# Second-sort sums, payloads and bucket comparisons in other places of a 32-slot neighbour-sum kernel, and two results turned by TensorE

## The chip, the cores and the metric

The kernel runs on one core of a Trainium2 chip. The metric is the device time of one execution in microseconds (us). Engines are called TensorE (PE in the profile; its weight loads are PEld), VectorE (DVE), ScalarE (ACT), GpSimd (POOL) and SyncE (SP).

## The reference, cut to what matters

```python
num_nodes, num_edges, dim = 4096, 65536, 128
output = np.zeros((num_nodes, dim), dtype=np.float32)
for i in range(len(edge_index_src)):
    output[edge_index_dst[i]] += node_features[edge_index_src[i]]
```

Every edge adds the feature row of its source node to the row of its destination node.

## The kernel before, in words

The nodes are 32 blocks of 128. The edges are sorted twice on the chip by prefix counts and permutation matmuls: a first sort by destination block, and then a second sort by source block inside each destination block. The second sort is done for 8 groups g = 0 to 7 of four destination blocks. The main loop has 32 slots; slots 4g to 4g+3 belong to group g, and each takes eight of the 32 source blocks.

**A slot.** VectorE writes one-hot matrices `oh` of low source and low destination numbers one slot ahead (`onehots(slot+1)`, L241), in two buffers. TensorE multiplies them into eight blocks `psa`, each of which counts the edges from one source block to the group's 512 destination nodes (L806, two halves of 16 matmuls), ScalarE casts each block to SBUF as `a` (L808), and TensorE multiplies features by `a` into the result bank `pso` (L813, eight products with k 0 to 3 in the slot itself, eight with k 4 to 7 in the next slot). TensorE's order in a slot is: first half of the blocks; place 2; the late products of the slot before; second half of the blocks; places 3 and 4; the early products; `finish`; place 5. VectorE's order is: place 0; the one-hots of the next slot; place 1; the later places. In slots before 5 the one-hots come in two halves, later in one.

**Hooks.** `at(slot, place, functions)` hangs the second sort's steps of a group into those places, by hand. Each engine runs what it is handed in this order, so a step that waits holds all that was handed to its engine after it. For a group g of 3 and up, with f = 4g:

- `buckets` (VectorE, L633): one-hot of the source block. `chunk_sums` (GpSimd, L653): adds it up in twos and fours, into `two` and `four`. The payloads that are owed by group g-1 (GpSimd, L642) follow.
- `before_all` (TensorE, L662, three matmuls into `psb`; ScalarE copies it out as `base`, L664): the sums ahead of each bucket. It reads `four`.
- `masked` and `folded` (GpSimd, L689, L696, L698): reads `base`.
- `payloads` (GpSimd, L642), by `LATE_PAYLOADS` here or owed to the next group.
- `repeats` (VectorE, L669, L675) and `repeats_folded` (GpSimd, L684).
- `ranks` (TensorE L706, ScalarE L710), which reads what `folded` and `repeats_folded` left; `permutations` (VectorE, L241, tiles `p2a` for even and `p2c` for odd groups); `permuted` (TensorE, L722); `quad_keys` (VectorE, L529).

Groups 1 and 2 have places of their own: group 2's `buckets` and `chunk_sums` stand inside `onehots(0)`, and its `before_all`, `masked` and `folded` in slot 0, behind `x_part(3, 1)` (GpSimd, L230).

**Results.** A result of four destination blocks is complete in slot 4k+4. ScalarE copies it from `pso` to the PSUM bank `misc` (`psx`, L376), VectorE transposes it in squares of 32 (`finish`, L390), and SyncE's queue stores it with four DMAs that put the squares in place. The last result goes out by `leave` (L397). The bank `misc` also takes `psb`; the bank `ps2` takes the ranks and the permuted pairs.

Of the kernel before, what the change touches and what calls it, by code (L numbers as in the profile page):

```python
# [8 lines left out]
P = 128  # L9
F32 = mybir.dt.float32  # L10
# [15 lines left out]
BIG = 4096.0  # L26
GROUPS = (4,) * 8
WARM = 38
LATE_PAYLOADS = (2, 3, 4, 5)

WIN = ((0, 4, 0, 44), (4, 9, 0, 72), (9, 13, 8, 92), (13, 17, 16, 112), (17, NJ, 28, P))

# [44 lines left out]
def _fast(ctx, tc, X, src32, dst32, out, ident, fmax, flag_i, T):  # L77
    nc = tc.nc
    V, S, G, PE = nc.vector, nc.scalar, nc.gpsimd, nc.tensor
# [3 lines left out]
    sb1 = ctx.enter_context(tc.tile_pool(name="sb1", bufs=1))  # L83
    sb2 = ctx.enter_context(tc.tile_pool(name="sb2", bufs=2))
    ps = ctx.enter_context(tc.tile_pool(name="ps", bufs=2, space=bass.MemoryType.PSUM))
# [12 lines left out]
    for a, b in runs:  # L98
        at, n = 8 * sum(QN[:a]), 4 * QN[a]
        for queue, of, to in ((nc.sync, dst32, rawd), (nc.scalar, src32, raws)):  # L100
            queue.dma_start(
                out=to.rearrange("p (q n) w -> p q n w", q=NQ)[:, a:b, :n],
                in_=bass.AP(of, at, [[2 * T, P], [2 * n, b - a], [2, n], [1, 2]]))
# [119 lines left out]
    def x_part(i, v, hs=(0, 1)):  # L223
        blks = slice(i % 2 * BX, (i % 2 + 1) * BX)
        if v == 0:
            S.copy(out=xr[i // 2][:, blks, 0, :], in_=xf[i])
        else:
            for h in hs:
                bs = slice(i % 2 * BX + h * BX // 2, i % 2 * BX + (h + 1) * BX // 2)
                G.tensor_tensor(out=xr[i // 2][:, bs, 1, :], op=OP.subtract,  # L230
                                in0=xf[i][:, h * BX // 2:(h + 1) * BX // 2],
                                in1=xr[i // 2][:, bs, 0, :])
# [139 lines left out]
    done = []  # L372

    def evacuate(k, pso):
        res = ps.tile([P, 512], F32, name="psx", tag="misc", bufs=1)
        S.copy(out=res[:], in_=pso[:])  # L376
        done.append((k, res))

    def store_blocks(queues, rows, k):

        for a in range(4):
            queues[a % len(queues)].dma_start(
                out=out[4 * k * P:4 * (k + 1) * P, 32 * a:32 * (a + 1)].rearrange(
                    "(b j) f -> j b f", j=32),
                in_=rows[32 * a:32 * (a + 1)].rearrange("p (b f) -> p b f", f=32))

    def finish():
        for k, res in done:
            rows = sb2.tile([P, 512], F32, name="rows", bufs=1)
            V.transpose(out=rows[:], in_=res[:])  # L390
            store_blocks((nc.sync,), rows, k)
        done.clear()

    def leave(k, pso):
# [206 lines left out]
    owed = {}  # L601
    hooks = {}

    def at(slot, where, *fs):
        hooks.setdefault((slot, where), []).extend(fs)

    def do(slot, where):
        for f in hooks.pop((slot, where), ()):
            f()

    def pass2(g):
# [43 lines left out]

        def before_all():
            T2["b"] = sb2.tile([P, 2, P], BF16, name="base2")
            psb = ps.tile([P, 512], F32, name="psb", tag="misc", bufs=1)
            of = T2["four"][:].rearrange("p (h i) w -> p h i w", h=2)
            n = NH // 4  # L660
            for i in range(n):
                PE.matmul(out=psb[:, :2 * P], lhsT=before[:], rhs=of[:, :, i],  # L662
                          start=i == 0, stop=i == n - 1)
            S.copy(out=T2["b"][:].rearrange("p h w -> p (h w)"), in_=psb[:, :2 * P])  # L664
# [48 lines left out]
        def permutations(j):  # L713
            pair_onehot(p2b[d0 // 2 % 4 + j], T2["r"][:, j], slice(0, NCH))

        def permuted(j):
            if j == 0:
                T2["ps2"] = ps.tile([P, 512], F32, name="ps2", tag="ps2", bufs=1)
            ps2 = T2["ps2"]
            for c in range(NCH):  # L720
                at = (c // NH * 2 + j) * 64
                PE.matmul(out=ps2[:, at:at + 64], lhsT=p2b[d0 // 2 % 4 + j][:, c, :],  # L722
                          rhs=T2["v"][:, c, :, 2 * j:2 * j + 2],
                          start=c % NH == 0, stop=c % NH == NH - 1)
            if j == 1:
                take_pairs(ps2[:, 8 * NB:8 * NB + P], ps2[:, :8 * NB])
# [32 lines left out]
        def each(*fs):  # L759
            return lambda: [f() for f in fs]  # L760
# [5 lines left out]
            return buckets, payloads, column_sums, sums_to_each, counts  # L766
        if g == 2:
            owed[2] = payloads
            at(1, 1, repeats, repeats_folded)
            at(4, 3, ranks, lambda: permutations(0), lambda: permutations(1))  # L770
            at(5, 3, lambda: permuted(0))
            at(5, 5, lambda: permuted(1))
            at(7, 0, quad_keys)
            return buckets, chunk_sums, before_all, each(masked, folded)
        f = 4 * g
        where = 4 if g == 3 else 1
        at(f - 10, where, buckets, chunk_sums, owed.pop(g - 1, lambda: None))
        at(f - 9, 5, before_all)
        at(f - 8, where, masked, folded)
        if g in LATE_PAYLOADS:  # L780
            owed[g] = payloads
        else:
            at(f - 8, where, payloads)
        at(f - 6, 1, repeats, repeats_folded)
        at(f - 4, 5, ranks)
        at(f - 3, 1, lambda: permutations(0), lambda: permutations(1))
        at(f - 3, 5, lambda: permuted(0), lambda: permuted(1))
# [2 lines left out]
    def onehots(slot):  # L790

        oh = sb1.tile([P, 2, 4 * 8, P], BF16, name="oh", tag=f"t2{slot % 2}")
        at = slot % 4 * 32
        parts = ((0, 16), (16, 16)) if slot < 5 else ((0, 32),)
        for i, n in ((0, 8), (8, 8), (16, 16)) if slot == 0 else parts:
            if i == 16 and slot == 0:
                buckets_2()
                chunk_sums_2()
            for k, io in ((0, piotas), (1, piota)):
                onehot(oh[:, k, i:i + n], keys2[slot // 4][k][:, at + i:at + i + n], n, io=io)  # L800
        return oh

    def blocks(k, oh, a):
        psa = ps.tile([P, 512], F32, name="psa", tag="psA", bufs=4)
        for i in range(4):
            PE.matmul(out=psa[:, i * P:(i + 1) * P], lhsT=oh[:, 0, 4 * k + i, :],  # L806
                      rhs=oh[:, 1, 4 * k + i, :], start=True, stop=True)
        S.copy(out=a[:, k, :], in_=psa[:])  # L808

    def product(k, slot, a, pso):  # L810
        s = slot % 4 * 8 + k
        for v in range(2):
            PE.matmul(out=pso[:], lhsT=xr[s // 16][:, s % 16, v, :], rhs=a[:, k, :],  # L813
                      start=s == 0 and v == 0, stop=s == NB - 1 and v == 1)
# [16 lines left out]
    def flag_of_all(fall):  # L831
        psf = ps.tile([P, 512], F32, name="psf", tag="misc", bufs=1)
        PE.matmul(out=psf[:1, :1], lhsT=fall[:], rhs=one[:], start=True, stop=True)
        V.tensor_single_scalar(out=flag_i[:], in_=psf[:1, :1], scalar=float(P * T),
                               op=OP.not_equal)

    buckets_1, payloads_1, column_sums_1, sums_1, counts_1 = pass2(1)
    buckets_2, chunk_sums_2, before_all_2, masked_counts_2 = pass2(2)
    for g in range(3, len(GROUPS)):
        pass2(g)  # L840

    V.tensor_copy(out=earlier[:, :, :4 * (NH - 1)].bitcast(F32),
                  in_=ones[:, :4 * (NH - 1)].bitcast(F32)[:, None].to_broadcast([P, 2, 2 * (NH - 1)]))
# [39 lines left out]
    for slot in range(slots):  # L883
        do(slot, 0)
        cur = oh
        if slot + 1 < slots:
            oh = onehots(slot + 1)
        do(slot, 1)
        a = sb1.tile([P, 8, 4 * P], F32R, name="a", tag=f"A{slot % 2}")
        if slot % 4 == 0:  # L890
            pso = ps.tile([P, 512], F32, name="pso", tag="pso", bufs=1)
        if slot == 0:
            for i in range(2):
                next(counting_1)
            for k in range(4):
                blocks(k, cur, a)
            for k in range(4):
                product(k, slot, a, pso)
                next(counting_1, None)
            x_part(3, 1)  # L900
            before_all_2()
            masked_counts_2()
        else:
            for k in range(4):
                blocks(k, cur, a)
        do(slot, 2)
        if slot > 1:
            for k in range(4, 8):
                product(k, *prev)
            if prev[0] % 4 == 3:  # L910
                evacuate(prev[0] // 4, prev[2])
        for k in range(4, 8):
            blocks(k, cur, a)
        do(slot, 3)
        do(slot, 4)
        for k in range(4, 8) if slot == 0 else range(4):
            product(k, slot, a, pso)
        finish()
        do(slot, 5)
        prev = (slot, a, pso)  # L920
        if slot == slots - 4:
            fall = flag()
        if slot == slots - 2:
            flag_of_all(fall)
# [93 lines left out]
```

## Time and profile before

| what | value |
|---|---|
| median of three runs | 281.36 us (280.43 to 281.39) |
| the profiled execution's own time | 280.37 us |
| its span, first to last instruction | 278.7 us |
| TensorE busy | 252.3 us, 91% |
| VectorE busy | 243.3 us, 87% |
| GpSimd busy | 197.0 us, 71% |
| ScalarE busy | 188.8 us, 68% |
| TensorE's mean granted clock | 0.977 |

The busy times are of the whole span. The span has a first part, the first sort, to about 54 us, and then the 32 slots. A busy share says little about which engine sets the pace in a stretch; the timelines of each engine do, with the idle time in front of an instruction and what ended it in square brackets. Rows of a timeline merge instructions of one kind, and matmuls overlap, so a cost is taken from the start of a row to the start of the next.

### The profile page before, as it was taken

The numbers are of one execution on the slowest core, as the hardware profiler recorded it, in microseconds if no ns is written. First come the engines' busy times: TensorE is split into PE (matmuls) and PEld (weight loads), VectorE is DVE, ScalarE is ACT, GpSimd is POOL, SyncE is SP. The second block draws the span as 40 slices with busy tenths as digits, with TensorE's granted clock in tenths as the row PEclk, the third lists the DMA queues.
The fourth block names the chain that finished last, engine by engine and source line by source line (L and its number), as shares of the span: only waits on it lengthen the run. The fifth ranks groups of instructions, "written<-read, shape, count | busy, mean of one in ns | idle before, by whom it ended". The sixth has DMA issues, their size and how long they took to land.

```text
span 278.7 us, 7494 instructions
## 1 busy us (share of the span) xinstructions
PE 252.3 (91%) x3148; PEld 211.2 (76%) x3148; DVE 243.3 (87%) x272; ACT 188.8 (68%) x433; POOL 197.0 (71%) x205
## 2 busy tenths in 40 slices
PE   8899998862999998899999999997699999999991
PEld 7789996641987786688878887885588878878880
DVE  7999979992899799999999999999389989988801
ACT  3799897560776756576877677675376776877750
POOL 5499999999986994999799989999899200000000
PEclk9999999996899999999999999999799999999998
DMA  5900000000000020001002000200020001002002
GB/s 161 289 7 6 2 6 2 2 1 0 2 0 4 2 36 4 0 12 28 2 0 40 0 4 5 37 2 0 0 41 0 2 15 25 2 1 40 0 1 41
DMA packets 22724, 5.75 MB, mean 21 GB/s; under 512 B 17056, under 2 KB 22688, under 8 KB 22688
## 3 DMA queue, kind: packets, MB, share of 16 engines
q1 hardware_dynamic: 20816, 4.59, 8.1%
q10 hardware_dynamic: 1872, 0.66, 1.1%
q8 instruction: 25, 0.41, 0.6%
q14 instruction: 11, 0.09, 0.1%
HBM read 3.15 MB, written 2.10 MB: 19 GB/s over the span
## 4 chain that ended last, share of the span: by engine, by line
PE 41%; DVE 24%; POOL 21%; ACT 7%; issue 5%; DVEq 0%; POOLq 0%
PE pso L813 20%; DVE oh L241 14%; PE psa L806 11%; POOL v L642 6%; POOL two L653 5%; ACT cum L283 4%; DVE p2a L241 3%; POOL four L653 3%; POOL cum L689 2%; POOL xr L230 2%; PE psm L364 2%; PE ps L722 2%; PE psw L144 2%; DVE oh L633 1%; DVE p2c L241 1%
## 5 line engine op out<-in xcount | busy, mean ns | idle before, releaser
L808 ACT CAST a<-psa 128x512 fp32r<-128x512 f32 x256 | 131.8, 604 | 28.5 <-PE psa L806 28.1
L813 PE MATMUL pso<-a,xr 128*128 128x512 f32 x512 | 135.4, 406 | 0.0
L813 PEld LDWEIGHTS pso<-a,xr 128*128 128x128 f32 x512 | 92.0, 190 | 16.7
L241 DVE TENSOR_TENSOR oh<-psi,slo 128x4096 bf16<-128x4096 uint16 (+2 forms) x38 | 73.7, 1940 | 7.3 <-PE psa L806 7.3
L241 DVE TENSOR_TENSOR oh<-psi,dlo 128x4096 bf16<-128x4096 uint16 (+2 forms) x38 | 73.8, 1943 | 0.0
L806 PE MATMUL psa<-oh 128*128 128x128 bf16 x1024 | 70.0, 222 | 2.2 <-DVE oh L241 2.2
L806 PEld LDWEIGHTS <-oh 128*128 128x128 bf16 x1024 | 59.6, 99 | 15.0 <-issue 11.0
L642 POOL TENSOR_TENSOR v<-oh,sa 128x512 bf16<-128x512 bf16 x42 | 42.6, 1055 | 0.0
L689 POOL TENSOR_TENSOR cum<-oh,base 128x512 bf16<-128x512 bf16 x36 | 40.7, 1175 | 1.4 <-ACT base L664 1.4
L339 POOL TENSOR_TENSOR v<-oh,kab 128x704 f32<-128x704 bf16 x24 | 32.8, 1401 | 5.6 <-ACT kab L217 5.3
L241 DVE TENSOR_TENSOR p<-psi,rank 128x352 bf16<-128x352 uint16 (+5 forms) x60 | 25.9, 499 | 1.8 <-ACT rank L304 1.7
L653 POOL TENSOR_TENSOR two<-oh 128x512 bf16<-128x512 bf16 x18 | 20.4, 1165 | 3.3 <-PE psa L806 3.3
L364 PE MATMUL psm<-v,p 128*128 128x64 bf16 x512 | 19.6, 193 | 0.9 <-DVE p L241 0.6
L283 ACT ACTIVATE cum<-psc,sums 128x256 bf16<-128x256 f32 x50 | 19.1, 553 | 0.5 <-PE psc L280 0.5
L364 PEld LDWEIGHTS <-p 128*128 128x128 bf16 x512 | 17.1, 98 | 2.1 <-DVE p L241 1.7
L684 POOL TENSOR_TENSOR same<-same 128x480 bf16<-128x480 bf16 (+1 forms) x12 | 9.9, 827 | 9.6 <-DVE same L675 9.1
L662 PE MATMUL psb<-four,before 128*128 128x256 bf16 x18 | 3.5, 314 | 14.2 <-POOL four L653 14.2
L241 DVE TENSOR_TENSOR p2a<-psi,rank 128x3072 bf16<-128x3072 uint16 (+2 forms) x14 | 14.2, 1061 | 2.0 <-ACT rank L710 2.0
L664 ACT CAST base<-psb 128x256 bf16<-128x256 f32 x6 | 2.2, 372 | 19.8 <-PE psb L662 19.8
L662 PEld LDWEIGHTS <-before 128*128 128x128 bf16 x18 | 1.8, 102 | 16.1 <-issue 16.0
L241 DVE TENSOR_TENSOR p2c<-psi,rank 128x3072 bf16<-128x3072 uint16 x8 | 13.6, 1745 | 0.0
L278 PE MATMUL psc<-early,oh 128*128 128x256 bf16 x67 | 13.2, 272 | 0.0
(113 smaller groups left out, 264.7 us busy)
## 6 DMA issues: line engine op xcount, KB each, us to landing
xf<-in_node_features_dram SPq DMA_DIRECT2D x4, 512.0 KB, 5.7
out_dram<-rows SPq DMA_DIRECT2D x30, 64.0 KB, 2.0
raw<-in_edge_index_src_dram ACTq DMA_DIRECT2D x1, 336.0 KB, 4.7
raw<-in_edge_index_dst_dram SPq DMA_DIRECT2D x1, 336.0 KB, 4.9
raw<-in_edge_index_src_dram ACTq DMA_DIRECT2D x2, 88.0 KB, 2.5
raw<-in_edge_index_dst_dram SPq DMA_DIRECT2D x2, 88.0 KB, 2.6
out_dram<-rows ACTq DMA_DIRECT2D x2, 64.0 KB, 2.9
```

Of the source, the lines that this page charges most:

```text
L241: V.tensor_tensor(out=dst.rearrange("p i (m k) -> p i m k", k=2), in0=io.rearrange("p i (m k) -> p i m k", k=2), in1=keys2[:, :, None, :]. ...
L278: PE.matmul(out=psc[:, at:at + 2 * P], lhsT=oh[:, 2 * i], rhs=early2[:], start=True, stop=False)
L283: S.activation(out=cum[:, 2 * i:2 * i + 2].rearrange("p j e -> p (j e)"), in_=psc[:, 2 * i * P:2 * (i + 1) * P], func=RELU, bias=bias)
L339: G.tensor_tensor(out=v1[q][:, l::4], in0=oh1q(q)[:, l::4], op=OP.mult, in1=kab[:, q, l::4, None].to_broadcast([P, NJ, NB]))
L364: PE.matmul(out=psm[:, l * 64:(l + 1) * 64], lhsT=t[:, j, l % 2, :], rhs=v1[q][:, 4 * j + l].bitcast(BF16), start=j == 0, stop=j == n - 1)
L642: G.tensor_tensor(out=T2["v"][:, c:c + 4], in0=T2["o"][:, c:c + 4], op=OP.mult, in1=sa[:, c:c + 4, None, d0:d0 + 4].to_broadcast([P, 4, NB ...
L653: G.tensor_tensor(out=to[:, js], in0=of[:, js, 0], in1=of[:, js, 1], op=OP.add)
L684: G.tensor_tensor(out=t[:, :, :n], in0=t[:, :, :n], in1=t[:, :, n:2 * n], op=OP.add)
L689: G.tensor_tensor(out=flat("c")[:, c:c + 4], in0=flat("o")[:, c:c + 4], op=OP.mult, in1=T2["b"][:, c // NH, None].to_broadcast([P, 4, P]))
L806: PE.matmul(out=psa[:, i * P:(i + 1) * P], lhsT=oh[:, 0, 4 * k + i, :], rhs=oh[:, 1, 4 * k + i, :], start=True, stop=True)
L808: S.copy(out=a[:, k, :], in_=psa[:])
L813: PE.matmul(out=pso[:], lhsT=xr[s // 16][:, s % 16, v, :], rhs=a[:, k, :], start=s == 0 and v == 0, stop=s == NB - 1 and v == 1)
```

## The change

Group 2's `before_all`, `masked`, `folded` and `repeats_folded` go from slots 0 and 1 to place 5 of slot 1. For group 3 and up `before_all` goes from place 5 of slot f-9 to place 2 of slot f-8, and `masked` and `folded` to the same place. Its bank is `ps2` and no longer `misc`. `buckets` and `chunk_sums` of groups 5 to 7 go from slot f-10 to slot f-11; `repeats` and `repeats_folded` from slot f-6 to f-7. The payloads of group 6 are owed to group 7, so that they stand behind group 7's `chunk_sums`. Results 0 and 2 are copied to SBUF (`res`), turned by four TensorE transposes into `misc`, copied to `rows` by ScalarE and stored with one DMA.

```diff
-LATE_PAYLOADS = (2, 3, 4, 5)
+LATE_PAYLOADS = (2, 3, 4, 5, 6)
+BY_TENSOR = (0, 2)
...
     def evacuate(k, pso):
-        res = ps.tile([P, 512], F32, name="psx", tag="misc", bufs=1)
+        if k in BY_TENSOR:
+            res = sb1.tile([P, 512], F32, name="res", tag="K1")
+        else:
+            res = ps.tile([P, 512], F32, name="psx", tag="misc", bufs=1)
         S.copy(out=res[:], in_=pso[:])
...
         for k, res in done:
-            rows = sb2.tile([P, 512], F32, name="rows", bufs=1)
-            V.transpose(out=rows[:], in_=res[:])
-            store_blocks((nc.sync,), rows, k)
+            if k not in BY_TENSOR:
+                rows = sb2.tile([P, 512], F32, name="rows", bufs=1)
+                V.transpose(out=rows[:], in_=res[:])
+                store_blocks((nc.sync,), rows, k)
+                continue
+            psx = ps.tile([P, 512], F32, name="psx", tag="misc", bufs=1)
+            for i in range(4):
+                PE.transpose(psx[:, i * P:(i + 1) * P], res[:, i * P:(i + 1) * P], ident[:])
+            rows = sb2.tile([P, 4, P], F32, name="rows", bufs=1)
+            S.copy(out=rows[:].rearrange("p i f -> p (i f)"), in_=psx[:])
+            nc.sync.dma_start(
+                out=out[4 * k * P:4 * (k + 1) * P, :].rearrange("(i p) f -> p i f", p=P),
+                in_=rows[:])
...
-            psb = ps.tile([P, 512], F32, name="psb", tag="misc", bufs=1)
+            psb = ps.tile([P, 512], F32, name="psb", tag="ps2", bufs=1)
...
         if g == 2:
             owed[2] = payloads
-            at(1, 1, repeats, repeats_folded)
+            at(1, 1, repeats)
+            at(1, 5, before_all, masked, folded, repeats_folded)
...
-            return buckets, chunk_sums, before_all, each(masked, folded)
+            return buckets, chunk_sums
         f = 4 * g
-        where = 4 if g == 3 else 1
-        at(f - 10, where, buckets, chunk_sums, owed.pop(g - 1, lambda: None))
-        at(f - 9, 5, before_all)
-        at(f - 8, where, masked, folded)
+        first_step = {3: (2, 4), 4: (6, 1)}.get(g, (f - 11, 1))
+        at(*first_step, buckets, chunk_sums, owed.pop(g - 1, lambda: None))
+        at(f - 8, 2, before_all, masked, folded)
         if g in LATE_PAYLOADS:
             owed[g] = payloads
         else:
-            at(f - 8, where, payloads)
-        at(f - 6, 1, repeats, repeats_folded)
+            at(f - 8, 2, payloads)
+        at(f - 7, 1, repeats, repeats_folded)
...
             x_part(3, 1)
-            before_all_2()
-            masked_counts_2()
```

## Rows read from the trace of the kernel before

**Rows 1.** Waits, longest first: in total us, times, longest us.
```profile
PE psb L662 <- POOL four L653: 14.2, 6, 7.7
```
**Rows 2.** Timeline of TensorE: start us, us, operation [idle before <-releaser].
```profile
60.18 0.39 PE L753 MATMUL psc<-identb,sums 128*128 128x128 bf16 x4
...
68.22 0.80 PE L662 MATMUL psb<-four,before 128*128 128x256 bf16 x3 [7.65 <-POOL four L653]
...
105.98 1.07 PE L806 MATMUL psa<-oh 128*128 128x128 bf16 x16 [1.19 <-DVE oh L241]
...
197.67 0.80 PE L662 MATMUL psb<-four,before 128*128 128x256 bf16 x3 [4.50 <-POOL four L653]
198.27 1.91 PE L806 MATMUL psa<-oh 128*128 128x128 bf16 x16
199.94 2.60 PE L813 MATMUL pso<-a,xr 128*128 128x512 f32 x8
202.38 1.07 PE L806 MATMUL psa<-oh 128*128 128x128 bf16 x16
```
**Rows 3.** The page's slices of about 7 us: TensorE's granted clock in tenths.
```profile
PEclk9999999996899999999999999999799999999998
```
**Rows 4.** Timeline of TensorE, steady slots: what each kind of step costs.
```profile
95.27 0.33 PE L706 MATMUL psr<-cum,identb 128*128 128x96 bf16 x4
...
95.60 2.10 PE L813 MATMUL pso<-a,xr 128*128 128x512 f32 x8
...
152.56 1.07 PE L806 MATMUL psa<-oh 128*128 128x128 bf16 x16
153.43 2.10 PE L813 MATMUL pso<-a,xr 128*128 128x512 f32 x8
155.37 1.61 PE L722 MATMUL ps<-v,p2a 128*128 128x64 bf16 x48
156.82 1.05 PE L806 MATMUL psa<-oh 128*128 128x128 bf16 x16
```
**Rows 5.** Timeline of GpSimd, slots 0 to 4.
```profile
70.54 6.79 POOL L689 TENSOR_TENSOR cum<-oh,base 128x512 bf16<-128x512 bf16 x6
...
80.98 1.72 POOL L684 TENSOR_TENSOR same<-same 128x480 bf16<-128x480 bf16 x2
86.03 3.41 POOL L653 TENSOR_TENSOR two<-oh 128x512 bf16<-128x512 bf16 x3 [3.33 <-PE psa L806]
...
91.14 6.09 POOL L642 TENSOR_TENSOR v<-oh,sa 128x512 bf16<-128x512 bf16 x6
```
**Rows 6.** Timeline of VectorE.
```profile
70.76 1.23 DVE L241 TENSOR_TENSOR oh<-psi,slo 128x2048 bf16<-128x2048 uint16 x1 [6.27 <-PE psa L806]
...
75.42 0.21 DVE L669 COPY psi<-sbk 128x48 f32<-128x48 f32 x1
...
76.35 3.41 DVE L241 TENSOR_TENSOR p2c<-psi,rank 128x3072 bf16<-128x3072 uint16 x2
...
84.21 1.75 DVE L633 TENSOR_TENSOR oh<-psi,sbk 128x3072 bf16<-128x3072 uint16 x1
85.87 0.41 DVE L529 TENSOR_SCALAR slo<-ps 128x256 uint16<-128x256 uint16 x1
...
97.50 3.42 DVE L241 TENSOR_TENSOR p2a<-psi,rank 128x3072 bf16<-128x3072 uint16 x2 [1.96 <-ACT rank L710]
100.84 0.70 DVE L390 STREAM_TRANSPOSE rows<-psx 128x512 f32<-128x512 f32 x1
...
143.04 2.28 DVE L241 TENSOR_TENSOR oh<-psi,slo 128x4096 bf16<-128x4096 uint16 x1
145.24 2.28 DVE L241 TENSOR_TENSOR oh<-psi,dlo 128x4096 bf16<-128x4096 uint16 x1
...
272.88 0.72 DVE L397 STREAM_TRANSPOSE rows<-pso 128x512 f32<-128x512 f32 x1 [7.40 <-PE pso L813]
```
**Rows 7.** Groups by line: xcount | busy us, mean ns | idle before us.
```profile
L813 PEld LDWEIGHTS pso<-a,xr 128*128 128x128 f32 x512 | 92.0, 190 | 16.7
```

More of the change, by code (lines that the diff above doesn't have):

```diff
@@ L837, in _fast @@
     buckets_1, payloads_1, column_sums_1, sums_1, counts_1 = pass2(1)
-    buckets_2, chunk_sums_2, before_all_2, masked_counts_2 = pass2(2)
+    buckets_2, chunk_sums_2 = pass2(2)
     for g in range(3, len(GROUPS)):
```

## The prediction

> **What bounds the kernel now.** I read the list of waits first, then the timeline of each engine through the 32 slots, then the page's clock line. The longest wait on TensorE is for `four`: 14.2 us, in six `before_all` steps [rows 1]. TensorE's timeline places it: 7.65 us in slot 0, 4.50 us at the end of slot 19 [rows 2]. The granted clock dips at just these two places [rows 3]. The second dip has a price: after the wait the three `psb` matmuls take 0.60 us, the 16 block matmuls 1.67 and the eight products 2.44 [rows 2], where steady slots take 0.87 for such blocks and 1.94 for such products [rows 4]; with half of 0.60 for `psb` that is 0.30 + 0.80 + 0.50 = 1.6 us lost. I take the same for the first dip.
>
> Between the dips no engine has much room. From rows 4 and 6, start to start: a slot costs TensorE 2 x (0.87 + 1.94) = 5.62 us; ranks add 0.33, the 48 permutation matmuls 1.45, `psb` 0.30. Four slots are 24.56. VectorE needs 2 x 2.20 = 4.40 for a slot's one-hots, and for each group 3.34 for two permutations, 0.93 for `repeats`, 1.66 for `buckets`, about 0.66 for `quad_keys` and 0.63 for the transpose (its 0.70 less the overlap): 24.8 for four slots. So from slot 6, where TensorE waits for one-hots for 1.19 us [rows 2], VectorE leads by a hair; when its group steps have run out, TensorE alone sets the end at 272.88, where the last transpose has waited for it [rows 6]. What a saved wait is worth thus depends on whether VectorE and GpSimd can follow.
>
> **Part by part.** I follow the new order in the old trace's time. A hand-over that is waited for gets 0.1 us at the end.
>
> *Slots 0 and 1.* Without `before_all` in slot 0, TensorE goes on at 60.4 (60.18 and the 0.2 until its successor could start) [rows 2]. The rest of slot 0 takes 0.87 + 1.94, slot 1 5.62 without late products, 3.68, and 32 rank matmuls, 4 x 0.33: 68.2. That is when `four` of group 2 is ready (`psb` started on it at 68.22), so the moved `before_all` waits for nothing, and `psb` ends at 68.5. GpSimd is busy with `x_part` until 70.54, when `masked` starts [rows 5]; `base` is there by then. So GpSimd's work for group 2 ends at 82.70 (80.98 + 1.72) as now: the move costs it nothing.
>
> *Slots 2 to 4: the wait comes back.* VectorE was free at 64.49 (70.76 less 6.27) and waited for a one-hot buffer [rows 6]; that buffer is now free about 61.5. It runs unbroken: one-hots of slot 2 (four pieces of 1.13, 1.23 less the overlap) to 69.0, `repeats` 69.9, permutations 73.3, one-hots of slot 3 77.8, `buckets` of group 3 79.4, keys 80.1, first half of slot 4's one-hots 82.4. TensorE does slot 2 (5.62 + 1.45) by 75.6 and slot 3 by 81.2, waits for those one-hots, and has slot 4's first blocks at 83.3. Now comes group 3's `before_all`, at place 2. GpSimd is free for group 3's sums at 82.70, not at 86.03 (the 3.33 us of idle time before them go) [rows 5], and they take 5.11 (86.03 to 91.14): `four` at 87.8. TensorE waits 4.6 us, and behind it stand slot 3's late products, result 0, the second half of slot 4 and the ranks of group 2, for which VectorE's permutations wait. The wait is as long as the one of 4.50 us that ended in the low clock, so I charge the 1.6 us too. This is the dearest unknown: between 0 (the 1.19 us wait in rows 2 shows no dip in rows 3) and 1.6.
>
> *Slots 4 to 8.* Ranks start at 87.9 + 0.30 + 1.94 + 0.87 + 1.6 = 92.6; before, at 95.27, with the permutations 2.23 us later at 97.50 [rows 4, 6]. So the permutations start at 94.8, 2.7 us sooner. Result 0's transpose leaves VectorE (0.63): slot 6's one-hots are ready 3.3 us sooner, and slot 6 starts at 102.7 against 105.98. TensorE with its turned result is there at 102.7 too. Then VectorE does `repeats`, one-hots 7, `buckets` 4, keys, one-hots 8: 12.05 us, to 114.65. TensorE has done slots 6 and 7 at 113.95 and waits 0.7. The sums of group 4 are ready at 114.7 (`buckets` at 109.6, and 5.11), TensorE asks at 115.6: no wait.
>
> *Slots 8 to 20.* Slot 8 takes 5.62 + 0.30 + 0.33, slot 9 7.07, slot 10 5.62: TensorE is at slot 11 at 133.6. With `repeats` and `buckets` a slot sooner, slot 11's one-hots come behind them: 114.65 + 3 x 4.40 + 0.63 + 3.34 + 0.93 + 1.66 = 134.4, a wait of 0.8. Slot 12 at 140.0 carries a turned result, which here is all on TensorE's path: slots 12 to 15 take 24.6 + 0.75 and no one-hots are late, so slot 16 is at 165.3. By the same sums slot 19 is reached at 184.2 and its one-hots are there at 184.6 (result 3's transpose waits for ScalarE's copy in slot 16). Slot 20 starts at 190.2, not at 198.27. GpSimd needs, for one group, 12.2 (70.54 to 82.70), 5.1 and 6.1 [rows 5] = 23.4 us in some 24.6 to 25.3: with group 6's payloads behind group 7's sums, no `four` is asked for before it is there, and the 4.50 us go with their dip.
>
> *After slot 20.* Before, 272.88 - 198.27 = 74.61. Less the dip (1.3 of it after 198.27), plus `psb` inside the slot: 73.6. The end is 263.8, with four hand-overs 264.2: 8.7 us sooner. Payloads of group 7 now behind its masks end near 208 (`before_all` in slot 20 at 191, then 10.4 and 6.1) and are needed in slot 25, near 226, so that move costs nothing; without those 18 us it would cost TensorE up to 6.1 us.
>
> *Turned results.* The trace shows no TensorE transpose. Four times 128 columns at the blocks' rate (0.87 / 16) are 0.22 us, the lower bound; the nearest row is the fp32 weight load, 0.19 us [rows 7], and 16 of these (four passes for each) are 3.0, the upper one. I take one load each, 0.75, since a 128-column matmul is too short to hide it. ScalarE's second copy of a result (some 0.7 us, as VectorE's move of the same size in rows 6) is taken at nothing, since ScalarE is busy for 68% of the span; without that cover it would hold up the casts behind it by as much. One DMA in place of four on SyncE's queue: nothing waits for it but the next result, four slots on.
>
> The Trainium skill (TensorE: Matmul & The Clock Gate, Part 4: PE-mode transpose) gives about 275 ns for a bf16 transpose of 128x128 inside a kernel and 390 alone. As an estimate that is 1.1 to 1.6 us for a result, and the sum would be 0.4 to 0.8 us later. Its page VectorE: DVE Perf Modes (The three transpose paths) has VectorE cheaper than TensorE for such a tile, which speaks against this part of the change; no run yet shows it here.
>
> `ps2` for `psb`: it must wait until `quad_keys` has read the bank, in slot f-9 and ahead of one-hots that slot f-8 needs anyway, so it is free in time.
>
> The sum is 280.37 - 8.7 = 271.7. The profiled execution is 1 us under the median of the runs (281.36) and close to the lowest (280.43), so I say **272.0**.
>
> **Rivals.**
> *The wait does not come back, or hardly.* If `four` of group 3 were there at 83.3, the permutations would start when VectorE is free, at 89.0 instead of 94.8: 266. For: VectorE and TensorE have both got that far by then. Against: GpSimd has no idle time in the rows up to 82.70, so nothing can bring its 5.11 us forward.
> *VectorE sets the pace.* If slots 11, 15 and 19 each waited for the full `repeats` and `buckets`, 2.59 us, instead of 0.8, 0 and 0.4, that is 6.6 us more: 278.3. For: 24.2 to 24.8 against 24.6 is close. Against: TensorE gets the turned result's time on top in slot 12. A milder form: group 3's sums start no sooner than 86.03, the wait is 3.3 us longer, 275.
> *Slower: turning on TensorE.* Beyond 0.75 us, a turned result's first 1.5 us are hidden in slots 8 and 11 for result 0 and 0.4 for result 2. For a time 0.5% above the old (281.8), with e us beyond for each, 2e - 1.9 = 10.1, e = 6: 6.7 us for each result, 1.7 us for each transpose. At 7 us it would be 282.3. For: four matmuls with fp32 loads in a row, each behind its own load, and the whole slot behind them. Against: even 16 loads are 3.0, which makes 274.3.
> *It comes to nothing:* the saved waits return in the same sum at slots 8, 12, 16; no row has GpSimd that late: 281.
>
> **How the numbers follow.** Forecast, 270 to 273.5 (without the dip 270.4; the turned result from 0.22 to 1.6): 0.64. No wait: 0.12. VectorE's pace or a longer wait, 273.5 to 278.3: 0.18. Nothing: 0.03. Slower: 0.03. Half a per cent is 1.4 us, about what a measurement tells from no change. The range, 268.5 to 276.5, takes in the forecast, its bounds with 16 loads (274.3) and 1 us of run difference, the longer wait, and leaves out most of the no-wait case and the full pace case. Faster 0.94, same 0.03, slower 0.03.
>
> **What would show it.** Slot 0 without a wait of TensorE for `four`, slot 4 with one of 4 to 5 us, and a dip of the clock behind it or not; group 3's sums starting on GpSimd at 82 to 83; short waits for one-hots at slots 8, 11 and 19; no wait at slot 19's end; slot 20 near 190; transposes of about 0.2 us each. Wrong it would be if TensorE waited long for one-hots after slot 8, if transposes took over 0.5 us each, or if GpSimd's steps came late at slots 8 to 20.

## The result, and the profile after

The changed kernel takes 271.76 us (median of four runs, 271.74 to 271.83); the kernel before, timed beside it, took 280.89 us (280.31 to 281.39). The ratio is 0.9676, 95% interval 0.9651 to 0.9701: 3.2% faster, and 0.2 us under the forecast of 272.0. The profiled execution took 271.77 us with a span of 270.2. Medians and ratios below leave out two executions that lie far from the rest of their sets, one of 403.9 us with `repeats` moved back and one of 616.69 us of the kernel before.

Two lines from the list of waits of the changed kernel (us in total, times, longest), and the page's clock line. Its line numbers differ from those above: the blocks are L820 and the products L827 (L806 and L813 before), the sums L667 (L653), `before_all` L676 (L662), the ranks L720 and L724 (L706 and L710), the one-hots L242 (L241).

```profile
DVE p2a L242 <- ACT rank L724: 5.9, 1, 5.9
...
PE psb L676 <- POOL four L667: 4.3, 1, 4.3
```
```profile
PEclk9999999999998699999999999999999999999997
```

Six waits of TensorE for `four`, 14.2 us [rows 1], have become one of 4.3. Two dips of the clock [rows 3] have become one, at 81 to 95 us (slices of 6.75 us). (The last slice is lower too, in both kernels; TensorE's last product ends in it.) TensorE's timeline shows where (the answer to [rows 2]):

```profile
68.87 0.50 PE L676 MATMUL psb<-four,before 128*128 128x256 bf16 x3
...
87.90 0.80 PE L676 MATMUL psb<-four,before 128*128 128x256 bf16 x3 [4.32 <-POOL four L667]
88.35 3.76 PE L827 MATMUL pso<-a,xr 128*128 128x512 f32 x8
91.91 1.43 PE L820 MATMUL psa<-oh 128*128 128x128 bf16 x16
93.18 0.33 PE L720 MATMUL psr<-cum,identb 128*128 128x96 bf16 x4
...
95.43 0.60 PE L400 MATMUL psx<-ident,res 128*128 128x128 f32 x4
95.87 1.06 PE L820 MATMUL psa<-oh 128*128 128x128 bf16 x16
...
102.94 1.05 PE L820 MATMUL psa<-oh 128*128 128x128 bf16 x16
...
115.18 1.07 PE L820 MATMUL psa<-oh 128*128 128x128 bf16 x16 [0.84 <-DVE oh L242]
...
135.12 1.07 PE L820 MATMUL psa<-oh 128*128 128x128 bf16 x16 [0.71 <-DVE oh L242]
...
185.26 1.07 PE L820 MATMUL psa<-oh 128*128 128x128 bf16 x16 [0.49 <-DVE oh L242]
...
190.89 1.07 PE L820 MATMUL psa<-oh 128*128 128x128 bf16 x16
191.79 0.49 PE L676 MATMUL psb<-four,before 128*128 128x256 bf16 x3
```

Group 2's `before_all` at 68.87 and group 7's at 191.79 wait for nothing. Group 3's, in slot 4, waits 4.32 us, and what follows it is slow: from 87.90 on, `psb` takes 0.45 us, the eight products 3.56 and the blocks 1.27, against 0.25, 1.94 and 0.87 in full clock. The windows of busy time by stretch (start and end, length, then TensorE, its weight loads, VectorE, ScalarE, GpSimd, the granted clock, and the DMA's share and GB/s) show the clock in it:

```profile
83.60:87.90 4.30, 0.00 (x1) 0.00 (x0) 4.30 (x3) 1.40 (x3) 4.30 (x6) 0.76 0.00 0
87.90:92.50 4.60, 4.60 (x17) 3.36 (x17) 1.21 (x1) 0.73 (x2) 4.60 (x5) 0.50 0.00 0
```

TensorE idles in the first stretch, and in the second its clock is at 0.50, the lower of its two levels (1.2 GHz), throughout. GpSimd is busy in both without a gap; its timeline says with what (the answer to [rows 5]):

```profile
81.05 1.72 POOL L698 TENSOR_TENSOR same<-same 128x480 bf16<-128x480 bf16 x2
82.73 3.38 POOL L667 TENSOR_TENSOR two<-oh 128x512 bf16<-128x512 bf16 x3
86.07 1.77 POOL L667 TENSOR_TENSOR four<-two 128x384 bf16<-128x384 bf16 x2
87.81 6.08 POOL L656 TENSOR_TENSOR v<-oh,sa 128x512 bf16<-128x512 bf16 x6
```

It takes up group 3's sums at 82.73, where in the kernel before it idled 3.33 us until 86.03 [rows 5], and cannot finish them before 87.8. VectorE (the answer to [rows 6]) then waits for the ranks behind all this, and the last transpose shows the end, 264.45 against 272.88:

```profile
95.04 3.42 DVE L242 TENSOR_TENSOR p2a<-psi,rank 128x3072 bf16<-128x3072 uint16 x2 [5.93 <-ACT rank L724]
...
264.45 0.72 DVE L411 STREAM_TRANSPOSE rows<-pso 128x512 f32<-128x512 f32 x1 [7.40 <-PE pso L827]
```

### The profile page after: what moved, and what is told of

Same layout as the page of the kernel before. It is cut to its first block, busy times and chain, and to the rows that moved or that the text cites. A ratio compares the mean times of both kernels' runs of the same rounds, so it can differ in the third digit from the quotient of the medians.

```text
span 270.2 us, 7501 instructions
## 1 busy us (share of the span) xinstructions
PE 252.3 (93%) x3155; PEld 210.7 (78%) x3156; DVE 242.1 (90%) x270; ACT 189.4 (70%) x435; POOL 197.0 (73%) x205
## 4 chain that ended last, share of the span: by engine, by line
PE 54%; POOL 18%; DVE 17%; ACT 7%; issue 2%; DVEq 0%; POOLq 0%; ACTq 0%
PE pso L827 29%; PE psa L820 14%; DVE oh L242 10%; POOL cum L703 5%; ACT cum L284 4%; POOL xr L231 3%; POOL two L667 2%; POOL v L656 2%; PE ps L736 2%; PE psm L365 2%; PE psw L145 2%; POOL cum L710 1%; DVE oh L647 1%; POOL four L667 1%; DVE p2c L242 1%
## 5 line engine op out<-in xcount | busy, mean ns | idle before, releaser
L827 PE MATMUL pso<-a,xr 128*128 128x512 f32 x512 | 136.3, 408 | 0.1
L827 PEld LDWEIGHTS pso<-a,xr 128*128 128x128 f32 x512 | 92.1, 191 | 17.4 <-ACT a L822 0.8
L242 DVE TENSOR_TENSOR oh<-psi,slo 128x4096 bf16<-128x4096 uint16 (+2 forms) x38 | 73.8, 1943 | 1.5 <-PE psa L820 1.5
L242 DVE TENSOR_TENSOR oh<-psi,dlo 128x4096 bf16<-128x4096 uint16 (+2 forms) x38 | 73.9, 1945 | 0.0
L820 PE MATMUL psa<-oh 128*128 128x128 bf16 x1024 | 68.8, 220 | 3.6 <-DVE oh L242 3.5
L820 PEld LDWEIGHTS <-oh 128*128 128x128 bf16 x1024 | 58.2, 98 | 17.7 <-issue 11.3
L242 DVE TENSOR_TENSOR p<-psi,rank 128x352 bf16<-128x352 uint16 (+5 forms) x60 | 26.0, 500 | 1.8 <-ACT rank L305 1.7
L667 POOL TENSOR_TENSOR two<-oh 128x512 bf16<-128x512 bf16 x18 | 20.4, 1160 | 4.2 <-DVE oh L647 4.2
L242 DVE TENSOR_TENSOR p2a<-psi,rank 128x3072 bf16<-128x3072 uint16 (+2 forms) x14 | 14.2, 1062 | 5.9 <-ACT rank L724 5.9
L242 DVE TENSOR_TENSOR p2c<-psi,rank 128x3072 bf16<-128x3072 uint16 x8 | 13.6, 1745 | 0.0
L647 DVE TENSOR_TENSOR oh<-psi,sbk 128x3072 bf16<-128x3072 uint16 (+3 forms) x9 | 12.5, 1393 | 0.0
L281 PE MATMUL psc<-early,oh 128*128 128x128 bf16 x67 | 12.1, 219 | 0.0
L710 POOL TENSOR_TENSOR cum<-cum 128x384 int32<-128x384 int32 x12 | 11.9, 1012 | 0.0
L535 ACT COPY ps<-ps 64x128 f32<-64x128 f32 x8 | 1.9, 235 | 13.8 <-issue 12.2
```

What stands on the lines that cost most here:

```text
L242: V.tensor_tensor(out=dst.rearrange("p i (m k) -> p i m k", k=2), in0=io.rearrange("p i (m k) -> p i m k", k=2), in1=keys2[:, :, None, :]. ...
L647: V.tensor_tensor(out=T2["o"][:, c0:c1], op=OP.is_equal, in0=psi[:, 2].bitcast(U16).rearrange("p (s k) -> p s k", k=4)[:, None].to_broadca ...
L667: G.tensor_tensor(out=to[:, js], in0=of[:, js, 0], in1=of[:, js, 1], op=OP.add)
L710: G.tensor_tensor(out=t[:, cs, :n], in0=t[:, cs, :n], in1=t[:, cs, n:2 * n], op=OP.add)
```

## The experiments

The first theory is the prediction's: a wait that TensorE loses is worth only what GpSimd and VectorE let through, so the parts do not add up. The rival is that each wait counts for itself. The changed kernel itself was timed in the set of the result only; the runs below come from three other sets, each with the kernel before beside them. The lowest times of the kernel before are 280.29 to 280.37 us in all four sets, so differences of half a microsecond and more between sets can be read, smaller ones hardly.

**Group 2's steps back in slot 0.**
```diff
-            at(1, 1, repeats)
-            at(1, 5, before_all, masked, folded, repeats_folded)
+            at(1, 1, repeats, repeats_folded)
...
             x_part(3, 1)
+            before_all_2()
+            masked_counts_2()
```


> The changed kernel with group 2's sums, masks and folds back in slot 0. Theory (a saved TensorE wait is worth only what GpSimd and VectorE let through): the wait for four in slot 0 returns with 7 to 8 us and a dip of the clock, but the one in slot 4 (4.32 us and its dip) goes, as group 3's sums are then ready in time; 2 us slower than the changed kernel, near 273.9 us. Rival (each wait counts for itself): 7.7 us and 1.6 of dip are added, near 281 us.

Measured: 274.36 us (273.58 to 274.66; ratio to before 0.9752, 0.9707 to 0.9796), 2.6 us over the changed kernel. TensorE's timeline:
```profile
68.16 0.80 PE L676 MATMUL psb<-four,before 128*128 128x256 bf16 x3 [7.65 <-POOL four L667]
92.66 0.49 PE L676 MATMUL psb<-four,before 128*128 128x256 bf16 x3
```
The wait of 7.65 us is back and the one of 4.32 is gone. The rival is out: between this run and the changed kernel, one long wait is exchanged for a shorter one.

**Only group 2's steps moved, in the kernel before.**
```diff
-            at(1, 1, repeats, repeats_folded)
+            at(1, 1, repeats)
+            at(1, 5, before_all, masked, folded, repeats_folded)
...
-            before_all_2()
-            masked_counts_2()
```


> The kernel before with only group 2's sums, masks and folds moved to place 5 of slot 1. Theory: slot 0's wait goes, TensorE comes to the end of slot 3 at about 82 and waits there until 87.9, nearly 6 us, with the dip behind it; slots 6 on are VectorE's as before and the 4.5 us wait in slot 19 stays: only 1.4 us faster than before, near 279.5 us. Rival: the 7.65 us and the dip of 1.6 are gained, near 272 us.

Measured: 279.74 us against 281.57 of before (ratio 0.9948, 0.9924 to 0.9971). TensorE's timeline:
```profile
87.89 0.80 PE L662 MATMUL psb<-four,before 128*128 128x256 bf16 x3 [5.82 <-POOL four L653]
...
196.12 0.80 PE L662 MATMUL psb<-four,before 128*128 128x256 bf16 x3 [4.51 <-POOL four L653]
```
As the theory says: a wait of 5.82 us at the end of slot 3 takes the place of 7.65 us in slot 0, and only 1.8 us reach the end (0.8 to 2.1 by the interval).

**Only group 6's payloads behind group 7's sums, in the kernel before.**
```diff
-LATE_PAYLOADS = (2, 3, 4, 5)
+LATE_PAYLOADS = (2, 3, 4, 5, 6)
```


> The kernel before with only the payloads of group 6 put behind group 7's sums. Theory: the wait of 4.5 us in slot 19 shrinks to some 0.4 us, and its dip of 1.6 us goes, with TensorE alone setting the pace after it, so all of it reaches the end: 6 to 6.5 us faster, near 274.5 us. Rival (VectorE, which is as busy there, takes the place of the wait): under 2 us, near 279.5 us.

Measured: 274.48 us against 281.57 (ratio 0.9766, 0.9724 to 0.9807), 7.1 us by the medians. The two traces differ by 5.9 us (last transpose at 266.98 and 272.88; the traced execution of the kernel before took 280.37 us), and that is the wait and its dip, 4.3 and 1.6. One line gives most of what the whole change gives. TensorE's timeline:
```profile
68.19 0.80 PE L662 MATMUL psb<-four,before 128*128 128x256 bf16 x3 [7.64 <-POOL four L653]
...
193.34 0.49 PE L662 MATMUL psb<-four,before 128*128 128x256 bf16 x3 [0.21 <-POOL four L653]
```
The early wait stays. The late one falls from 4.50 to 0.21 us, its dip is gone with it, and nothing later takes their place.

**The same line taken back out of the changed kernel.**
```diff
-LATE_PAYLOADS = (2, 3, 4, 5, 6)
+LATE_PAYLOADS = (2, 3, 4, 5)
```


> The changed kernel with the payloads of group 6 ahead of group 7's sums again. Theory: with buckets a slot sooner and before_all half a slot later, GpSimd has 5 us more before TensorE asks, so six more us of payloads ahead of four make it late by 0.3 us only, no dip: near 272.1 us. Rival (this line carries the gain in both kernels): 6 us slower, near 278 us.

Measured: 271.76 us (271.61 to 272.07), the changed kernel's own time. The line that gives 6 to 7 us alone is worth nothing here. GpSimd has group 7's sums ready 6 us later than in the changed kernel and still in time:
```profile
190.12 1.79 POOL L667 TENSOR_TENSOR four<-two 128x384 bf16<-128x384 bf16 x2
```
```profile
190.92 1.07 PE L820 MATMUL psa<-oh 128*128 128x128 bf16 x16
191.96 0.49 PE L676 MATMUL psb<-four,before 128*128 128x256 bf16 x3
```
(GpSimd's timeline, then TensorE's.) `four` is ready at 191.9 and `psb` starts at 191.96; asked for at the end of slot 19 (190.9), as before, it would have been 1.0 us late and not 4.5. The rest of the slack comes from GpSimd's own waits. In the kernel before it stood idle for `repeats` four times, with the next group's sums behind it; this is the line from its list of waits, and then the only one of this kind in the run below with `repeats` back at its old slot but `buckets` a slot sooner:

```profile
POOL same L684 <- DVE same L675: 9.1, 4, 4.0
```
```profile
POOL same L698 <- DVE same L689: 4.2, 1, 4.2
```

In the run with the payloads moved back, and in the changed kernel, there is none. This points to the earlier `buckets` for more than half of the idle time that is gone; the later `before_all` adds the 0.9 us of slot 20's first blocks. Neither was tried alone. The two cures of the late wait, the payloads' order and these moves, are alternatives and not terms of a sum.

**Group 3's sums asked for later in slot 4.**
```diff
-        at(f - 8, 2, before_all, masked, folded)
+        at(f - 8, 5 if g == 3 else 2, before_all, masked, folded)
```


> The changed kernel with group 3's before_all, masked and folded at place 5 of slot 4 in place of 2. Theory: four is ready when TensorE comes to it, so the 4.32 us wait and its dip go, and VectorE's permutations start 6 us sooner; about 1.3 us comes back as a wait for group 4's four in slot 8: 266 us. Rival (GpSimd sets the pace, so the wait only moves to slot 8): 270.5 to 271.8 us.

Measured: 266.58 us (266.55 to 266.63; ratio 0.9484, 0.9444 to 0.9524), 5.2 us under the changed kernel. TensorE's timeline:
```profile
88.97 0.49 PE L676 MATMUL psb<-four,before 128*128 128x256 bf16 x3
...
111.18 0.49 PE L676 MATMUL psb<-four,before 128*128 128x256 bf16 x3 [0.93 <-POOL four L667]
```
The late products, the second half of the blocks and the ranks run while GpSimd adds; the wait and its dip are gone, and 0.93 us comes back in slot 8. The rival, that GpSimd sets the pace, is out.

**The clock kept up through the wait of slot 4.**
```diff
+        if g == 3:
+            at(f - 8, 2, lambda: keep_busy(70))
         at(f - 8, 2, before_all, masked, folded)
```


> The changed kernel with 70 extra 128-column matmuls on TensorE just before group 3's before_all in slot 4, so that TensorE is busy for about 4 us of its wait; their result is not used. Theory: no dip of the clock after the wait; the steps behind it take 0.87 and 1.94 us again, and all of what the dip cost (2.2 us by the row of the products, 3.56 for 1.94, psb and blocks) reaches the end, as VectorE waits for the ranks: near 269.6 us. Rival (VectorE's one-hots set slot 6 anyway, so the dip is hidden): 271.5 us or more.

Measured: 269.96 us (269.93 to 270.02; ratio 0.9604, 0.9577 to 0.9631), 1.8 us under the changed kernel. TensorE's timeline:
```profile
83.55 4.07 PE L145 MATMUL psw<-ones 128*128 128x128 bf16 x70
87.93 0.49 PE L676 MATMUL psb<-four,before 128*128 128x256 bf16 x3 [0.31 <-POOL four L667]
88.17 2.09 PE L829 MATMUL pso<-a,xr 128*128 128x512 f32 x8
90.10 1.07 PE L822 MATMUL psa<-oh 128*128 128x128 bf16 x16
```
`four` comes no sooner, at 87.9, but the products behind it take 1.93 us, not 3.56, and the window of this stretch has the clock at 1.00 throughout:

```profile
82.50:96.00 13.50, 13.18 (x155) 11.77 (x156) 9.39 (x6) 7.39 (x17) 13.50 (x14) 1.00 0.04 13
```

So the dip comes from the idle wait. Of its 2.2 us by the rows, 1.8 reach the end: TensorE's ranks come 2.17 us sooner (91.01 for 93.18), VectorE's permutations, which wait until ScalarE has passed the ranks on, only 1.85 (93.19 for 95.04), and VectorE's one-hots then set the start of slot 6, 1.87 us sooner (101.07 for 102.94).

**No result turned by TensorE.**
```diff
-BY_TENSOR = (0, 2)
+BY_TENSOR = ()
```


> The changed kernel with no result turned by TensorE. Theory: VectorE gets 0.63 us back on its list before slot 6 and again in slot 12, and TensorE loses 0.44 us of transposes in each; as VectorE's one-hots end the wait in slots 6, 8 and 11, result 0 counts: 0.8 us slower, near 272.5 us. Rival (the turned results cost TensorE what they save): within 0.2 us of 271.8.

Measured: 272.67 us (272.51 to 272.83; ratio 0.9703, 0.9675 to 0.9731), 0.9 us slower. Slot 6 waits for one-hots again:
```profile
91.65 1.08 PE L820 MATMUL psa<-oh 128*128 128x128 bf16 x16
92.57 0.34 PE L720 MATMUL psr<-cum,identb 128*128 128x96 bf16 x4
...
103.23 1.07 PE L820 MATMUL psa<-oh 128*128 128x128 bf16 x16 [1.14 <-DVE oh L242]
```
The size is not clean: here the dip cost less, the blocks behind it taking 0.92 us (91.65 to 92.57) and not 1.27, so the turned results may be worth up to half a microsecond more.

**Only the turned results, in the kernel before.** The diff is that of `evacuate` and `finish`, with `BY_TENSOR = (0, 2)`.

> The kernel before with only results 0 and 2 turned by TensorE. Theory: VectorE is ahead of the work from slot 6 to 19, so its 0.63 us before slot 6 comes through as an earlier slot 6, but GpSimd's sums of group 7 still end the wait in slot 19: 0.5 to 1.0 us faster than before. Rival (the 0.44 us on TensorE undo it): within 0.3 us of before.

Measured: 279.87 us against 280.87 (ratio 0.9952, 0.9930 to 0.9975): the turning helps by itself, by 1.0 us (0.7 to 2.0 by the interval). The two traces differ by only 0.3 us at the end: the sums of group 7 come 1.0 us sooner (`psb` in slot 19 at 196.66 for 197.67), but the dip behind them cost 0.7 us more in this execution.

**`repeats` a slot later again.**
```diff
-        at(f - 7, 1, repeats, repeats_folded)
+        at(f - 6, 1, repeats, repeats_folded)
```


> The changed kernel with repeats back in slot f-6. Theory: the waits for one-hots in slots 11 and 19 (0.71 and 0.49 us) shrink to some 0.2 us, since 0.93 us of VectorE's work no longer stands ahead of them, and repeats_folded is still in time on GpSimd: 0.8 us faster, near 271.0 us. Rival (the earlier repeats keep GpSimd from waiting, and chunk sums come late without them): slower, 272.5 us or more.

Measured: 270.62 us (270.33 to 270.80; ratio 0.9623, 0.9587 to 0.9658), 1.1 us faster than the changed kernel. Its timeline has no wait for one-hots in slots 11 and 19; the one in slot 8 stays, with 0.81 us. This part of the change costs time.

**The parts that the runs favour, together.**
```diff
-        at(f - 8, 2, before_all, masked, folded)
+        at(f - 8, {3: 5, 4: 3}.get(g, 2), before_all, masked, folded)
...
-        at(f - 7, 1, repeats, repeats_folded)
+        at(f - 6, 1, repeats, repeats_folded)
```


> The changed kernel with before_all, masked and folded of group 3 at place 5 of slot 4 and of group 4 at place 3 of slot 8, and repeats back in slot f-6. Theory: the gains of the three places add up only where TensorE's waits stand one after the other, which they do: group 3's place gave 5.2 us, group 4's takes the last 0.9 us wait for four, and repeats 1.0 us less one-hot wait, together 7 us under the changed kernel: near 264.6 us. Rival (GpSimd or VectorE is the bound from slot 8 on): 266 us or more.

Measured: 264.74 us (264.56 to 264.81; ratio 0.9426, 0.9390 to 0.9461), 7.0 us under the changed kernel and 5.7% under the kernel before. TensorE's timeline:
```profile
109.06 1.07 PE L820 MATMUL psa<-oh 128*128 128x128 bf16 x16 [0.83 <-DVE oh L242]
112.78 0.49 PE L676 MATMUL psb<-four,before 128*128 128x256 bf16 x3
```
The one-hots of slot 8 still come 0.83 us late; no `before_all` waits any more.

## Why the prediction was right, point by point

- **Slots 0 and 1.** `before_all` of group 2 without a wait, `psb` forecast to end at 68.5: it starts at 68.87 and the next blocks at 69.21. Right, 0.7 us late. Most of that lies in slot 0: ScalarE was moving out group 1's counts until 61.24, so its cast, and with it the products, came behind (61.76; the blocks ahead of them start at 60.35 and take 0.87 elsewhere). Nothing waited for it.
- **The wait comes back in slot 4.** Forecast 83.3 to 87.9, 4.6 us; measured 4.32, `psb` at 87.90. GpSimd's start was forecast at 82.70 and was 82.73. That the wait lies in the order of TensorE's steps and not in GpSimd's pace was shown by moving this one request (5.2 us).
- **The dip behind it** was charged at 1.6 us and called the dearest unknown. It came, and the rows make it 2.2 (0.20 + 1.62 + 0.40). Here the clock stood at 0.50 for the 4.6 us behind the wait; behind that in slot 19 of the kernel before, the same view gives 0.64 (197.67 to 202.27). The last section has more on this. The run with the clock kept up gives 1.8 us at the end.
- **Turned results** were mis-sized: 0.75 us was taken for each; four transposes take 0.44 (95.43 to 95.87). The fp32 weight load in the nearest row took 190 ns [rows 7], here 140, and the loads overlap the matmuls. So this term was 0.3 too dear where the dip's was 0.6 too cheap, and slot 6 came at 102.94, forecast 102.7: that two errors nearly cancel there is luck. ScalarE's second copy of a result, taken at nothing, took 0.59 us, and no step of TensorE waits behind it.
- **Slots 8, 11 and 19.** Waits for one-hots forecast 0.7, 0.8 and 0.4; measured 0.84, 0.71 and 0.49. That `repeats` ahead of the one-hots causes the second and the third was shown by moving it back; the first stayed, since there `repeats` comes ahead of slot 8's one-hots at either place.
- **The wait of slot 19** gone: right. But the text gave it to the payloads' order. That is the step that the prediction had wrong: the line is enough alone, but is not needed once `buckets` comes a slot sooner and `before_all` later, and taken back, it changed nothing. As either cure takes the whole wait away, the total did not suffer.
- **After slot 20.** Start 190.2 forecast, 190.89 measured; from there to the end 73.6 forecast, 73.56 measured. Total gain in the trace 8.43 us (272.88 to 264.45), forecast 8.7; by the medians 9.1.

The rivals: that the wait would not come back fell with slot 4's row; that VectorE sets the pace fell with waits of 0.5 to 0.8 and not 2.59 us; that the transposes are dear fell with 0.11 us each; that the waits come back at slots 8, 12 and 16 fell with the one wait for `four`. The new bank of `psb` was not tried by itself; no wait for it shows in TensorE's rows.

## What to carry to other kernels

In an in-order queue the place of a request matters as much as the time of its answer: put it behind everything that does not need the answer (5.2 us for one number in the code). Follow a removed wait through the next steps of every engine that feeds it, since a wait of 7.65 us taken out of slot 0 alone gave 1.8. Parts of a change may be alternatives: judge each both alone and by taking it out of the whole, as the payloads' line shows with 6 to 7 us and nothing.

## What the runs showed of the hardware

The TensorE transposes were cheaper than expected. One tile's view of the changed kernel (duration in ns, minimum, median and maximum):

```profile
L400 PEld LDWEIGHTS psx<-ident,res x8: 139/140/142, 95.2 to 146.8; 128*128 128x128 f32 x8
L400 PE MATMUL psx<-ident,res x8: 272/273/273, 95.4 to 146.9; 128*128 128x128 f32 x8
```

A record lasts 273 ns, but four of them pass in 0.44 us, 0.11 each, start to start. The Trainium skill (TensorE: Matmul & The Clock Gate, Part 4: PE-mode transpose) gives about 275 ns for one in a kernel; the records agree, for fp32 too, but that is the time of one and not its cost in a row. The comparison with VectorE in the Trainium skill (VectorE: DVE Perf Modes, The three transpose paths), which speaks for VectorE on a tile alone where squares of 32 are enough, as here, did not decide: VectorE's one instruction costs 0.63 us of a list that TensorE waits for, and the two runs, with the turning taken out and put in alone, put it at 0.9 and 1.0 us in TensorE's favour.

The cost of a low-clock stretch is not fixed by the wait ahead of it. After waits of 4.50 us in the kernel before and 4.32 us after the change, `psb`, products and blocks lost 1.6 and 2.2 us. Behind the wait of 4.51 us in the same slot 19, in the run with only group 2's steps moved, they lost 2.3 us (196.12 to 201.48, against 3.06 in full clock), and behind 4.36 us in the run without turned results 1.6. Windows show what differs, first in the kernel before (slot 19), then in the changed one (slot 4):

```profile
193.20:197.60 4.40, 0.00 (x0) 0.00 (x0) 4.25 (x2) 0.00 (x0) 4.40 (x5) 1.00 0.00 0
197.70:200.90 3.20, 3.20 (x21) 2.85 (x21) 0.00 (x0) 2.28 (x5) 1.89 (x2) 0.50 0.00 0
201.10:204.00 2.90, 2.90 (x26) 2.36 (x25) 0.78 (x2) 1.39 (x3) 2.90 (x4) 1.00 0.00 0
```
```profile
85.90:92.60 6.70, 4.70 (x18) 3.46 (x18) 3.21 (x2) 0.83 (x2) 6.70 (x8) 0.50 0.00 0
92.80:95.00 2.20, 2.20 (x25) 1.94 (x23) 0.00 (x0) 2.20 (x6) 2.20 (x4) 1.00 0.02 7
```

In the first the clock fell only as the wait ended, and TensorE worked at the low level for 3.3 us; in the second it fell 2 us before the wait ended, and TensorE worked at it for 4.7 us. Each loss, 1.6 and 2.2 us, is about half of the time worked at the low level. Why the clock falls at another point of the wait was not tried.
